# Seven products of quarters instead of eight in the second FFN's up projection

## The chip, the cores and the metric

The kernel runs on one core of one Trainium2 chip. Its metric is the device time of one execution in microseconds; the number that counts is the median of several runs. The core has a matrix engine (TensorE, PE in the rows, with its weight loads as PEld), three engines for element-wise work (VectorE, DVE; ScalarE, ACT; GpSimd, POOL), and an engine that issues the DMAs (SyncE, SP).

## The reference

The kernel computes a two-layer block over 512 latent tokens and 256 context tokens of 1024 channels, in float32. Layer 0 mixes by two convolutions, layer 1 by windowed attention; each is followed by a feed-forward network (FFN). The change is in the FFN of layer 1, which runs on the 512 latent tokens alone:

```
def conv_ffn(h, w_up, conv, w_down):
    u = dwconv(h @ w_up, conv)          # h: 512 x 1024, w_up: 1024 x 5632, three taps along the tokens
    a, g = jnp.split(u, 2, axis=-1)     # 2816 features each
    return (jax.nn.silu(g) * a) @ w_down
```

## The kernel before

Channels or features lie on the 128 partitions, tokens along the free dimension. `h` is 8 channel tiles of 512 tokens. The 5632 features of the up projection are 44 tiles of 128: pair f (0 to 21) is feature tile f of the half a and of the half g.

Every product in float32 is made of three: each operand is split into a high and a low part of at most twelve bits (`split`, lines 156 to 159: a cast on ScalarE, line 158, and a subtraction on VectorE, line 159), and `mm3` (lines 173 to 178) adds low x high, high x low and high x high into one accumulator in PSUM. So a feature tile of the up projection takes 8 channel tiles x 3 matmuls of 512 columns. Weights come by `weights` (line 161): a DMA of 128 x 1024 into one of three `wraw` buffers, then the split.

The second FFN is `ffn(1, ...)` from line 652, in the order of the program:

- The tokens come in two halves of 256. `output` and `tokens_in_turn` make `h` of the first half, then of the second (`mod_in`, line 330, with its VectorE and ScalarE steps), and prepare the weights of the first six feature tiles (pairs 0 to 2). `side_by_side` (line 200) makes these six for the first half of the tokens and then for the second, while `h` of the second half is still being made.
- `self.todo` holds the rest of the modulation: eight rows, each a DMA of 512 KB and a reduction on VectorE (line 253), which the gate of the down projection needs.
- `up(f)` (line 685) makes the two tiles of a pair, the weights one tile ahead; then three taps of the convolution for each tile (`conv3`: the middle tap out of PSUM by ScalarE, line 367, the two others by VectorE, line 369, their input in PSUM too), SiLU on ScalarE, the product on VectorE (line 704), and the split of the result g.
- `down(grp)` (line 707) projects a group of g back: groups are pairs 0–3, 4–7, 8–11, 12–16, 17–21. The projection of a group is written after the first pair of the next group. It has 8 output tiles of 4 or 5 x 3 matmuls of 512 columns, each with its own weights, and adds the gated result to x on VectorE (line 359). The last group's projection goes in two halves of tokens with the final norm.

Accumulators are eight PSUM slots of 512 columns, taken in turn. The order on each engine is not only that of the program: a planner goes through the instructions by its own estimates of their times, and gives an engine the first one in program order that it holds to be ready. `issue_after` ties an instruction behind another on its engine. Semaphores are then set for that order, and each engine's queue runs strictly in it.

## Time and profile before

| | us |
|---|---|
| median of 3 runs | 1493.58 |
| all runs | 1493.09, 1493.58, 1495.0 |
| span of the profiled execution | 1491.3 |
| TensorE busy | 1456.9 |
| VectorE busy | 1023.7 |
| ScalarE busy | 594.9 |
| GpSimd busy | 47.1 |

The profile is of one execution. Its span goes from the first to the last instruction; the page has no other time for that execution, and the median of the runs is 2.3 us above the span. A row of a timeline has the start and the duration of an instruction; of instructions that follow each other without a gap the next one starts some 0.07 us before the duration of the last one is over, so the time that an instruction takes up on its engine is read from start to start. The second FFN lies between 1109 us and the end.

### The profile page before, as it was taken

How to read it: one execution, taken by the hardware profiler on the slowest of the kernel's cores; microseconds unless marked ns; L12 is line 12 of the kernel's file. 1: busy time of each engine (PE TensorE's matmuls, PEld its weight loads, DVE VectorE, ACT ScalarE, POOL GpSimd, SP SyncE). 2: the span in 40 equal slices, each digit the busy share in tenths (PEclk: the TensorE clock that was granted, in tenths of full speed). 3: DMA queues.
4: the chain of work that ended last, by engine and by line, in shares of the span. 5: the costliest groups of instructions: out<-in, count | busy, mean ns of one | idle time of the engine just before them, and what ended most of it. 6: DMA issues, size and time to landing. Idle time of an engine off the chain costs nothing.

```text
span 1491.3 us, 21938 instructions
## 1 busy us (share of the span) xinstructions
PE 1456.9 (98%) x8786; PEld 1236.1 (83%) x8786; DVE 1023.7 (69%) x1635; ACT 594.9 (40%) x983; POOL 47.1 (3%) x186
## 2 busy tenths in 40 slices
PE   5999999999999999999999999999999999999998
PEld 4888888888888888888888878868799888888887
DVE  6699998679877756456434679786676854655455
ACT  5421224463213223123122376686664442424235
POOL 0000001110000000000000010110000000000000
PEclk9999999999999999999999999999999999999999
DMA  9314434034543532342211324011154333233222
GB/s 374 113 61 170 156 114 136 30 105 148 163 131 124 184 99 85 108 133 82 88 44 44 98 79 141 10 43 51 45 176 162 94 105 104 79 108 95 93 77 75
DMA packets 52709, 161.23 MB, mean 108 GB/s; under 512 B 6400, under 2 KB 6528, under 8 KB 52480
## 3 DMA queue, kind: packets, MB, share of 16 engines
q1 hardware_dynamic: 52608, 159.84, 32.6%
q8 instruction: 68, 1.11, 0.3%
q14 instruction: 33, 0.27, 0.1%
HBM read 155.10 MB, written 2.10 MB: 105 GB/s over the span
## 4 chain that ended last, share of the span: by engine, by line
PE 91%; DVE 3%; DMA 2%; ACT 2%; issue 1%; POOL 0%; DVEq 0%; ACTq 0%
PE slot L176 22%; PE slot L177 21%; PE slot L178 21%; PE av L177 3%; PE av L176 3%; PE av L178 3%; PE av L928 2%; PE pt L918 2%; PE s L899 2%; PE pt L176 2%; PE pt L177 2%; PE pt L178 2%; PE slot L225 1%; PE slot L211 1%; PE slot L207 1%; PE slot L208 1%
## 5 line engine op out<-in xcount | busy, mean ns | idle before, releaser
L176 PE MATMUL slot<-h,wlo 128*128 128x512 f32 (+1 forms) x1192 | 414.9, 350 | 2.2 <-DVE ub L569 1.1
L178 PE MATMUL slot<-h,whi 128*128 128x512 f32 (+1 forms) x1192 | 415.5, 349 | 0.0
L177 PE MATMUL slot<-h,whi 128*128 128x512 f32 (+1 forms) x1192 | 415.1, 349 | 0.2 <-DVE h L349 0.2
L158 ACT CAST whi<-wraw 128x1024 fp32r<-128x1024 f32 (+2 forms) x215 | 191.8, 900 | 210.6 <-PE slot L178 110.4
L176 PEld LDWEIGHTS slot<-h,wlo 128*128 128x128 f32 x1192 | 224.1, 188 | 37.3 <-issue 1.8
L177 PEld LDWEIGHTS slot<-h,whi 128*128 128x128 f32 x1192 | 225.1, 189 | 31.7 <-DVE h L349 0.5
L178 PEld LDWEIGHTS slot<-h,whi 128*128 128x128 f32 x1192 | 225.1, 189 | 30.5
L159 DVE TENSOR_TENSOR wlo<-wraw,whi 128x1024 fp32r<-128x1024 f32 (+2 forms) x215 | 222.0, 1038 | 23.8 <-ACT whi L158 23.3
L369 DVE SCALAR_TENSOR_TENSOR cf<-slot,par,cf 128x769 f32<-128x769 f32 (+1 forms) x132 | 122.0, 927 | 146.6 <-ACT cf L367 146.1
L176 PE MATMUL slot<-gh,wlo 128*128 128x512 f32 (+1 forms) x459 | 157.5, 344 | 0.4 <-DVE x L359 0.4
L367 ACT ACTIVATE cf<-slot,par 128x770 f32<-128x770 f32 (+1 forms) x66 | 55.0, 834 | 256.7 <-PE slot L178 244.1
L177 PE MATMUL slot<-gl,whi 128*128 128x512 f32 (+1 forms) x459 | 156.7, 342 | 0.0
L178 PE MATMUL slot<-gh,whi 128*128 128x512 f32 (+1 forms) x459 | 156.2, 341 | 0.0
L359 DVE SCALAR_TENSOR_TENSOR x<-slot,mod,x 128x256 f32<-128x256 f32 (+1 forms) x139 | 81.8, 617 | 81.0 <-PE slot L178 80.8
L577 DVE SCALAR_TENSOR_TENSOR cacc<-ub,par,cacc 128x783 f32<-128x783 f32 x120 | 118.3, 1035 | 0.2
L253 DVE CUSTOM_DVE_ANT_0 junk<-wmod,cb 128x1024 bf16<-128x1024 f32 x80 | 97.5, 1219 | 9.4 <-DMA wmod<-in_wmt 5.8
L176 PEld LDWEIGHTS slot<-gh,wlo 128*128 128x128 f32 x459 | 86.4, 189 | 12.3 <-issue 0.7
L177 PEld LDWEIGHTS slot<-gl,whi 128*128 128x128 f32 x459 | 86.6, 189 | 10.9 <-issue 0.2
L178 PEld LDWEIGHTS slot<-gh,whi 128*128 128x128 f32 x459 | 86.7, 189 | 10.5
L906 DVE CUSTOM_DVE_ANT_0 sm<-s,mask,nsink 128x640 f32<-128x640 f32 (+1 forms) x58 | 46.8, 819 | 16.0 <-PE pt L918 12.4
L703 ACT ACTIVATE sgf<-cf 128x770 f32<-128x770 f32 (+1 forms) x44 | 32.6, 741 | 61.3 <-DVE cf L369 61.1
L909 ACT ACTIVATE sm<-sm,nm 128x513 f32<-128x513 f32 (+1 forms) x64 | 50.0, 785 | 10.3 <-DVE nm L906 5.4
(244 smaller groups left out, 2247.0 us busy)
## 6 DMA issues: line engine op xcount, KB each, us to landing
wraw<-in_w_up SPq DMA_DIRECT2D x88, 512.0 KB, 3.4
wmod<-in_wmt SPq DMA_DIRECT2D x56, 512.0 KB, 3.9
wmod<-in_wm SPq DMA_DIRECT2D x40, 512.0 KB, 4.9
wraw<-in_w_down SPq DMA_DIRECT2D x48, 256.0 KB, 2.7
wraw<-in_w_in SPq DMA_DIRECT2D x20, 512.0 KB, 4.1
wraw<-in_w_down SPq DMA_DIRECT2D x32, 320.0 KB, 3.0
wraw<-in_w_o SPq DMA_DIRECT2D x16, 512.0 KB, 3.3
wraw<-in_w_out SPq DMA_DIRECT2D x16, 256.0 KB, 3.5
```

Of the source, the lines that this page charges most:

```text
L158: self.act_mark = self.nc.scalar.copy(hi, src)
L159: self.mark = self.nc.vector.tensor_tensor(lo, src, hi.bitcast(F32), op=ALU.subtract)
L176: mm(out, lo, xh, start=first, stop=False)
L177: mm(out, hi, xl, start=False, stop=False)
L178: self.product = mm(out, hi, xh, start=False, stop=last)
L253: nc.vector.tensor_tensor_reduce(junk, w, self.cb[:, c, :], 1.0, 0.0, ALU.mult, ALU.add, col)
L359: self.nc.vector.scalar_tensor_tensor(self.x[k][:, lo:hi], acc, self.mod[:, l, chunk * 8 + k, c:c + 1], self.x[k][:, lo:hi], op0=ALU.mult, ...
L367: nc.scalar.activation(acc[:, :n], u[:, :n], AF.Copy, scale=w[:, 1:2])
L369: nc.vector.scalar_tensor_tensor(acc[:, o], u[:, i], w[:, j:j + 1], acc[:, o], op0=ALU.mult, op1=ALU.add)
L577: self.tapped = nc.vector.scalar_tensor_tensor(acc, ub[:, t:t + CB_N], w[:, t:t + 1], acc, op0=ALU.mult, op1=ALU.add)
L906: scored = nc.vector.tensor_tensor_reduce(sm[:, :n], s[:, SEQ - nl:SEQ + CTX], mk, -SCALE, nsink[:, hd:hd + 1], ALU.add, ALU.min, nm)
L909: self.scored = scored, nc.scalar.activation(sm[:, :n + 1], sm[:, :n + 1], AF.Exp, scale=-1.0, bias=nm, accum_out=z)
```

## The change

For pairs 3 to 21 the up projection is written as a product of a 2 x 2 matrix of weight quarters and a 2 x 2 matrix of quarters of `h`: features of a or of g, by even or odd channel tiles, by the first or the second 256 tokens. The eight products of quarters (each 4 channel tiles x 3 matmuls of 256 columns) become Strassen's seven (in Winograd's form), of sums of quarters.

- `quarters` makes the sums of quarters of `h` once, from the unsplit `h`, which `mod_in` now writes into tiles that are kept (`raw`): for each of four pairs of channel tiles one subtraction of 512 elements, two of 256, and two splits of 512. It stands in the program before the rows of the modulation and before `side_by_side`.
- `load_seven` loads a pair's weights (one DMA of 512 KB and two of 256 KB) and makes four sums of weight quarters of 512 elements, two on VectorE and two on GpSimd.
- `split_seven` splits the seven weight quarters: three times 128 x 1024, once 128 x 512. The splits for the next pair are written between the products of the current one (`then`).
- `seven` makes the seven products in three PSUM slots of 256 columns, and combines them into two tiles in SBUF (`ua`, `ug`): four copies out of PSUM by ScalarE, three additions or subtractions with one operand in PSUM by VectorE. One accumulator takes up four of the products, and is read by ScalarE or VectorE between one and the next; another takes two. The three taps then read these tiles.
- The down projection's weights use two pairs of buffers in turn instead of up to five, and other buffers in the last projection. The loaded weights of these pairs are laid out with even channel tiles before odd ones. The scratch for dynamic DMAs is set to 1024 bytes.

Pairs 0 to 2 and all of layer 0 keep their operations. The diff also takes comments out, which is left out here:

```diff
...
-    def mm3(self, out, w, k, xh, xl, first, last):
+    def mm3(self, out, w, k, xh, xl, first, last, more=False):
         hi, lo = (t[:, k * P:(k + 1) * P] for t in w)
-        mm = self.nc.tensor.matmul
+        mm = partial(self.nc.tensor.matmul, skip_group_check=more)
...
-    def mod_in(self, h, k, r, n, l, shift, segs):
+    def mod_in(self, h, k, r, n, l, shift, segs, raw=None):
...
-        t = self.tmp.tile([P, T], F32, name="ht", tag="tC")
+        t = self.tmp.tile([P, T], F32, name="ht", tag="tC") if raw is None else raw(k, lo)
...
+    def load_seven(self, f):
+        nc = self.nc
+        w = self.a["w_up"][1][f]
+        ra, rb, rc = (self.wts.tile([P, 1024], F32, name="wraw", tag="wraw", bufs=3) for _ in range(3))
+        rd = self.ph.tile([P, 512], F32, name="wrd", tag="wrd")
+        nc.sync.dma_start(ra, w[0])
+        nc.sync.dma_start(rd, w[1][:, 512:])
+        nc.sync.dma_start(rc[:, 512:], w[1][:, :512])
+        nc.vector.tensor_tensor(rc[:, :512], ra[:, :512], ra[:, 512:], op=ALU.add)
+        nc.vector.tensor_tensor(ra[:, 512:], ra[:, 512:], rd, op=ALU.add)
+        nc.gpsimd.tensor_tensor(rb[:, :512], ra[:, 512:], ra[:, :512], op=ALU.add)
+        nc.gpsimd.tensor_tensor(rb[:, 512:], rb[:, :512], rc[:, 512:], op=ALU.add)
+        return ra, rb, rc, rd
+    def seven(self, f, parts, h, then):
+        nc = self.nc
+        xa, va, ya = (self.slot()[:, :256] for _ in range(3))
+        ua, ug = (self.ph.tile([P, SEQ], F32, name=n, tag=f"{n}{f % 2}") for n in ("ua", "ug"))
+        q = lambda t, i: t[:, 256 * i:256 * i + 256]
+        b = {n: [(q(x[0], i), q(x[1], i)) for x in src] for n, src, i in (
+            ("11", h[0::2], 0), ("21", h[1::2], 0), ("22", h[1::2], 1),
+            *((n, list(zip(self.th, self.tl)), i) for i, n in enumerate(("n1", "t3", "n2", "t4"))))}
+        lo, hi = slice(0, 256), slice(256, 512)
+        def product(acc, w, n, start=False):
+            for k in range(4):
+                self.mm3(acc, w, k, *b[n][k], start and k == 0, k == 3, not start)
+        (a11, s1), (s2, s4), (s3, a12), (a22,) = parts
+        product(xa, a11, "11", True)
+        nc.scalar.copy(ua[:, lo], xa)
+        product(va, s1, "n1", True)
+        nc.scalar.activation(ug[:, hi], va, AF.Copy, scale=-1.0)
+        then(0)
+        product(xa, s2, "n2")
+        nc.scalar.copy(ua[:, hi], xa)
+        product(va, s4, "22")
+        then(1)
+        product(xa, s3, "t3")
+        nc.vector.tensor_tensor(ug[:, hi], ug[:, hi], xa, op=ALU.subtract)
+        product(ya, a12, "21", True)
+        then(2)
+        product(xa, a22, "t4")
+        then(3)
+        nc.vector.tensor_tensor(ua[:, hi], ua[:, hi], va, op=ALU.add)
+        nc.vector.tensor_tensor(ua[:, lo], ua[:, lo], ya, op=ALU.add)
+        nc.scalar.activation(ug[:, lo], xa, AF.Copy, scale=-1.0)
+        return ua, ug
+    def late(self, i):
+        return [self.act.tile([P, DM], F32R, name=f"{t}{i}") for t in ("whi", "wlo")]
+    def quarter_room(self, p):
+        return [pool.tile([P, 1024], F32R, name=t, tag=f"{t}{p}") for t, pool in (("th", self.act), ("tl", self.ph))]
+    def halves(self, hi, lo):
+        return (hi[:, :512], lo[:, :512]), (hi[:, 512:], lo[:, 512:])
+    def split_seven(self, raws, i, first=False):
+        raw = raws[i]
+        if first:
+            out = []
+            for j in range(2):
+                hi, lo = (self.ph.tile([P, SEQ], F32R, name=t, tag=f"{t}{4 + j}") for t in ("gh", "gl"))
+                self.split(raw[:, 512 * j:512 * j + 512], hi, lo)
+                out.append((hi, lo))
+            return out
+        if i == 3:
+            hi, lo = (self.act.tile([P, DM], F32R, name=f"{t}2")[:, :512] for t in ("whi", "wlo"))
+            self.split(raw, hi, lo)
+            return [(hi, lo)]
+        hi, lo = (self.wts.tile([P, 1024], F32R, name=t, tag=t, bufs=3) for t in ("whi", "wlo"))
+        self.split(raw, hi, lo)
+        return self.halves(hi, lo)
...
-        # the first tiles take the first tokens while the others are not there yet
+        if l:
+            self.quarters()
         self.do(11 if l else 3)
         done = [self.slot() for _ in self.pre]
         self.side_by_side(done, h, segs)
         nf = len(done)
-        with self.tc.issue_after(self.marks[0].ins), self.tc.issue_after(self.marks[1].ins):
-            ahead = self.weights(a["w_up"][l, ups[nf][0], ups[nf][1]], into=self.spare(0))
+        if l == 0:
+            with self.tc.issue_after(self.marks[0].ins), self.tc.issue_after(self.marks[1].ins):
+                ahead = self.weights(a["w_up"][l, ups[nf][0], ups[nf][1]], into=self.spare(0))
+        else:
+            raws = self.load_seven(nf // 2)
+            self.parts = [self.split_seven(raws, i, i == 0) for i in range(4)]
         g = []
 
         def up(f):
-            nonlocal ahead
+            nonlocal ahead, raws
             acc = []
+            if l and 2 * f >= nf:
+                now = self.parts
+                if f + 1 < NF:
+                    raws = self.load_seven(f + 1)
+                    self.parts = []
+                def then(i):
+                    if f + 1 < NF:
+                        self.parts.append(self.split_seven(raws, i))
+                u = self.seven(f, now, h, then)
             for part in range(2):
                 i = 2 * f + part
                 if i < nf:
                     s = done[i]
+                elif l:
+                    s = u[part]
                 else:
                     w = ahead
                     if i + 1 < len(ups):
...
 
         def down(grp):
             for m in range(KT):
-                w = self.weights(a["w_down"][l][grp][m], len(GROUPS[grp]) * P, self.spare(m % 3) if m % 3 < 2 else None)
+                room = (self.spare(m % 3) if m % 3 < 2 else None) if l == 0 else self.late(m % 2)
+                w = self.weights(a["w_down"][l][grp][m], len(GROUPS[grp]) * P, room)
                 s = self.slot()
                 self.wide_gemm(s, w, g[GROUPS[grp][0]:GROUPS[grp][-1] + 1], whole)
                 for lo, hi in whole:
...
         for grp, fs in enumerate(GROUPS):
             for f in fs:
                 up(f)
-                # the last tile of a group is ready once the next group's first product is through
                 if grp and f == fs[0]:
                     down(grp - 1)
         self.do(len(self.todo))
...
             t = self.ph.tile([P, 2, DM], F32R, name="wcb", tag="cb")
             return t[:, 0, :], t[:, 1, :]
 
-        room = {4: partial(self.spare, 0), 5: partial(self.spare, 1), 7: cb}
-        room[6] = partial(self.spare, i, n, ("gh", "gl")) if l == 0 else partial(self.spare, 2)
+        if l == 0:
+            room = {4: partial(self.spare, 0), 5: partial(self.spare, 1), 7: cb}
+            room[6] = partial(self.spare, i, n, ("gh", "gl"))
+        else:
+            room = {4 + p: partial(self.quarter_room, p) for p in range(4)}
         project = self.project(wd, len(last) * P, last, segs, l, 5, lead=2, late=6, few=(2, 4), room=room)
         if l == 0:
             self.tokens_in_turn(segs, project, (2, 1, 0), [a["w_k"][0], a["w_k"][1], a["w_q"][0]])
...
                 slots = self.turned(segs[1])
             self.final(segs[1], slots, y1)
 
...
+        self.raw = [self.act.tile([P, 1024], F32, name="raw", tag=f"th{p}") for p in range(KT // 2)]
+        def raw(k, lo):
+            t = self.raw[k // 2]
+            if k % 2 == 0:
+                return t[:, 0:512]
+            return t[:, 768:1024] if lo == 0 else t[:, 256:768]
         half = self.project(a["w_o"], DM, o, HALVES[1:], 1, 2, few=(1, 3))
-        self.tokens_in_turn(HALVES, half, (3, 1, 3), [w[f, part] for f in range(3) for part in range(2)], 0, room)
+        self.tokens_in_turn(
+            HALVES, half, (3, 1, 3), [w[f, part] for f in range(3) for part in range(2)], 0, room, raw)
+        self.room = room
+    def quarters(self):
+        nc = self.nc
+        self.th, self.tl = [], []
+        for p, raw in enumerate(self.raw):
+            b = raw.rearrange("p (q n) -> p q n", q=4)
+            t, u = (self.tmp.tile([P, T], F32, name="qs", tag=g)[:, :SEQ] for g in ("tA", "tB"))
+            nc.vector.tensor_tensor(
+                t.rearrange("p (q n) -> p q n", q=2), b[:, 0:3:2, :], b[:, 1:2, :].broadcast_to([P, 2, 256]), op=ALU.subtract)
+            nc.vector.scalar_tensor_tensor(u[:, :256], t[:, :256], -1.0, b[:, 2, :], op0=ALU.mult, op1=ALU.subtract)
+            nc.vector.scalar_tensor_tensor(u[:, 256:], u[:, :256], -1.0, b[:, 3, :], op0=ALU.mult, op1=ALU.subtract)
+            hi, lo = self.quarter_room(p)
+            for i, src in enumerate((t, u)):
+                self.split(src, hi[:, 512 * i:512 * i + 512], lo[:, 512 * i:512 * i + 512])
+            self.th.append(hi)
+            self.tl.append(lo)
 
...
+    even_odd = d["w_up"][1, 3:].reshape(NF - 3, 2, P, KT // 2, 2, P).transpose(0, 4, 2, 1, 3, 5)
+    d["w_up"][1, 3:] = even_odd.reshape(NF - 3, 2, P, DM)
...
+    nc = bacc.Bacc("TRN2", target_bir_lowering=False, num_devices=1, dynamic_dma_scratch_size=1024)
```

## Rows read from the trace of the kernel before

**Rows 1.** Page, part 1: busy us and share of each engine over the span.

```profile
PE 1456.9 (98%) x8786; PEld 1236.1 (83%) x8786; DVE 1023.7 (69%) x1635; ACT 594.9 (40%) x983; POOL 47.1 (3%) x186
```

**Rows 2.** Busy time by stretch of the second FFN: us, then each engine's busy time (instructions).

```profile
1144.30:1166.99 22.69, 22.37 (x97) 17.85 (x96) 21.23 (x33) 12.66 (x20) 0.00 (x0) 1.00 0.50 154
...
1166.99:1450.00 283.01, 283.00 (x1223) 229.23 (x1222) 160.20 (x209) 97.39 (x136) 0.00 (x0) 1.00 0.30 94
```

**Rows 3.** Chain of waits from 1118 us: start, us, what.

```profile
1148.97 1.15 DVE wlo L159
```

**Rows 4.** Timeline of TensorE, second FFN: start, us, line, operation, out<-in.

```profile
1106.14 0.28 PE L176 MATMUL slot<-oh,wlo 128*128 128x256 f32 x1
...
1108.99 0.28 PE L207 MATMUL slot<-h,wlo 128*128 128x256 f32 x1
...
1155.14 0.40 PE L176 MATMUL slot<-h,wlo 128*128 128x512 f32 x1
...
1166.29 0.40 PE L176 MATMUL slot<-h,wlo 128*128 128x512 f32 x1
...
1172.77 0.63 PE L176 MATMUL av<-gh,wlo 128*128 128x512 f32 x2
```

**Rows 5.** Timeline of VectorE, back-to-back instructions at two places.

```profile
190.08 2.92 DVE L577 SCALAR_TENSOR_TENSOR cacc<-ub,par,cacc 128x783 f32<-128x783 f32 x3
192.91 0.95 DVE L600 TENSOR_TENSOR ya<-slot,acca 128x770 f32<-128x770 f32 x1
...
1148.88 1.22 DVE L159 TENSOR_TENSOR wlo<-wraw,whi 128x1024 fp32r<-128x1024 f32 x1
1150.02 1.40 DVE L369 SCALAR_TENSOR_TENSOR cf<-slot,par,cf 128x511 f32<-128x511 f32 x2
1151.34 1.22 DVE L159 TENSOR_TENSOR wlo<-wraw,whi 128x1024 fp32r<-128x1024 f32 x1
```

**Rows 6.** Timelines of GpSimd and VectorE where both work: a sum, then small operations.

```profile
193.07 1.89 POOL L583 TENSOR_TENSOR cs<-cacc 128x783 f32<-128x783 f32 x1 [149.98 <-DVE cacc L577]
...
193.78 2.96 DVE L577 SCALAR_TENSOR_TENSOR cacc<-ub,par,cacc 128x783 f32<-128x783 f32 x2
...
197.53 1.97 DVE L577 SCALAR_TENSOR_TENSOR cacc<-ub,par,cacc 128x783 f32<-128x783 f32 x2
...
1118.97 1.23 DVE L159 TENSOR_TENSOR wlo<-wraw,whi 128x1024 fp32r<-128x1024 f32 x1 [0.34 <-ACT whi L158]
...
1119.04 1.21 POOL L298 TENSOR_TENSOR rt<-rt,rv 128x2 f32<-128x2 f32 x1
...
862.59 2.79 POOL L298 TENSOR_TENSOR rt<-rt,rv 128x2 f32<-128x2 f32 x1
...
866.29 0.20 POOL L298 TENSOR_TENSOR rt<-rt,rv 128x2 f32<-128x2 f32 x1
...
864.03 0.68 DVE L349 TENSOR_TENSOR h<-ht,h 128x512 fp32r<-128x512 f32 x1
864.64 0.68 DVE L335 TENSOR_TENSOR xr<-x,r 128x512 f32<-128x512 f32 x1
```

**Rows 7.** ScalarE's groups by form: busy us, mean ns of one, then idle before.

```profile
L158 ACT CAST whi<-wraw 128x1024 fp32r<-128x1024 f32 x135 | 140.7, 1045 | 123.2 <-PE slot L178 65.2 <-DMA wraw<-in_w_up 39.4 <-issue 7.9
...
L367 ACT ACTIVATE cf<-slot,par 128x512 f32<-128x512 f32 x22 | 15.2, 689 | 45.9 <-PE slot L178 37.8 <-PE slot L211 8.1
...
L826 ACT COPY v<-slot 128x256 f32<-128x256 f32 x6 | 2.2, 363 | 1.4 <-PE slot L824 1.4
```

**Rows 8.** Page, part 6: DMA issues, KB each, median us to landing.

```profile
wraw<-in_w_down SPq DMA_DIRECT2D x48, 256.0 KB, 2.7
```

**Rows 9.** Timeline of VectorE, head of the second FFN.

```profile
1133.53 0.43 DVE L159 TENSOR_TENSOR h<-ht,h 128x256 fp32r<-128x256 f32 x1 [0.77 <-ACT h L158]
1135.90 1.22 DVE L253 CUSTOM_DVE_ANT_0 junk<-wmod,cb 128x1024 bf16<-128x1024 f32 x1 [1.95 <-ACT cb L665]
...
1177.89 0.68 DVE L159 TENSOR_TENSOR gl<-sgf,gh 128x512 fp32r<-128x512 f32 x1
```

More of the change, by code (lines that the diff above doesn't have):

```diff
@@ L351, in mod_in, with modulated @@
             self.split(t[:, lo:hi], h[k][0][:, lo:hi], h[k][1][:, lo:hi])
[L353 removed]
+    def modulated(self, h, r, n, l, shift, seg, raw=None):
         for k in range(KT):
[L355 removed]
+            self.mod_in(h, k, r, n, l, shift, [seg], raw)
     def gate_in(self, k, acc, l, chunk, lo, hi):
@@ L506, in layer0_output, with tokens_in_turn @@
         self.tokens_in_turn(segs, project, (1, 0, 3), [up[0, 0], up[0, 1], up[1, 0]], 3)
-    def tokens_in_turn(self, segs, project, norm, first, early=1, room=()):
+    def tokens_in_turn(self, segs, project, norm, first, early=1, room=(), raw=None):
         self.pre = [self.weights(w) for w in first[:early]]
```

7 lines of the change are left out of this document (2 added, 5 removed).

## Prediction

> **What bounds the kernel now.** I read the page's busy shares first, then the stretches of the second FFN, then the chain of waits, then the engines' timelines there. The page [rows 1] shows TensorE busy 98% of the span of 1491.3 us; the reader should see that VectorE is not idle beside it: 69% over all. By stretch [rows 2], between 1144.3 and 1167.0 us, where the second FFN has its six first tiles done and makes pairs 3 and 4, VectorE is busy 21.2 of 22.7 us, and over the rest, to 1450.0, 160.2 of 283.0. TensorE is busy throughout, at a granted clock of 1.00. So the stage is bound by the number of columns that TensorE streams, with VectorE close behind at its head. The chain of waits [rows 3] says the same: its last link outside TensorE before the tail is a split of weights on VectorE, from 1148.97 us; behind it stand matmuls alone.
>
> **What is removed: TensorE time.** A pair of tiles takes 48 matmuls of 512 columns; from 1155.14 to 1166.29 us [rows 4] that is 11.15 us, 0.232 each. After: 7 products x 4 tiles x 3 parts = 84 matmuls of 256 columns. Twenty-four of these, each with a weight load of its own as here, took 2.85 us from 1106.14 to 1108.99 [rows 4], 0.119 each: 10.0 us a pair. The shorter matmul already includes whatever its weight load costs, so the loads (84 for 48) are no further term. Saved: 1.15 us x 19 pairs (3 to 21) = 21.9 us, if TensorE never waits.
>
> **What is added on VectorE.** I take start-to-start times of back-to-back instructions, since a row's duration overlaps the next one's [rows 5]: 0.61 us for 512 elements of two SBUF tensors (864.03 to 864.64, rows 6), 1.14 for 1024 (1148.88 to 1150.02), so 0.34 for 256 by the slope; 0.66 for a tap of the FFN's convolution (two from 1150.02 to 1151.34). Taps now read SBUF instead of PSUM; three such of 783 elements took 2.83 us (190.08 to 192.91), 0.943 each, by the same slope 0.66 at 511, so no change. A pair then has two weight sums 1.22, three splits of 1024 and one of 512 4.03, three accumulations out of PSUM 1.02, four taps 2.64, product and split of g 1.22: 10.1 us. Before it was 2.28 + 2.64 + 1.22 = 6.1 of 11.15. So VectorE alone now needs as long as TensorE (10.0).
>
> **What is added on GpSimd, and its price on VectorE.** Two sums of 512 elements a pair. The one large GpSimd sum in the trace, 783 elements, took 1.89 us [rows 6], so 512 take about 1.24. That row also shows the price: it began at 193.07; the two taps that VectorE began at 193.78 took 2.96 us, where the two at 197.53 took 1.97. VectorE lost 0.99 of the 1.18 us that the sum still had. The other way round [rows 6], a product of two elements on GpSimd, 0.20 us alone (866.29), took 1.21 beside one split of 1024 (1118.97) and 2.79 beside VectorE's unbroken work, until 865.3. The two engines exclude each other on two-SBUF-tensor work. 1.12 us (1.24 x 1.70/1.89) is what a sum would cost VectorE from its first moment; where it starts beside an accumulation out of PSUM (one SBUF operand; the product at 192.91 [rows 5], one operand in PSUM, kept its 0.87 us to the next start) less. I take 0.95 a sum. Bounds: 0, if the sums find VectorE idle, and 3.7 us a pair, rival 2. A pair in steady state: 10.1 + 1.9 = 12.0 us, longer than the 11.15 of before.
>
> The Trainium skill ("SBUF — State Buffer", section "Who interferes with whom") speaks against the change in the same way: a VectorE instruction with two SBUF inputs and a GpSimd instruction that reads SBUF share a port, and whichever starts first blocks the other for its whole length. The trace agrees in kind (0.99 us lost, 2.79 for 0.20). By the rule in full, 1.24 a sum, a pair would take 12.6, twelve pairs of the runs below 0.6 us more each, and the time would be near 1512.
>
> **ScalarE and DMA.** ScalarE gets four casts of at most 1.05, four copies of 256 columns at 0.36, and keeps the pair's first taps, SiLU and g, four of about 0.69 [rows 7]: 8.4 us of 10, hidden. Each copy must end before its accumulator is used again one product (1.43 us) later; alone it does, queued behind a cast of 1.05 just about. Bytes are the same, 1 MB a pair. Queue: in SP's order the pair's DMAs (first rows whole, second in two halves) stand behind the release of raw buffers. The quarter d is released by its split at the start of a pair; cast and split at most 1.05 + 0.68, landing 2.7 for 256 KB, sum 0.68, cast 1.05, split 1.22 make 7.4 us [rows 5 to 8] before the next pair can start. Of the 2.6 us left I give 1.1 to hand-overs and queues: VectorE may lag 1.5 us in a run of pairs before TensorE stops.
>
> **The sum by stretch.** The projections down stand after pairs 4, 8, 12, 17, and VectorE has slack there; the last pair's convolution (3.84) and its sums fall into it. So pairs come in runs. The first of a run needs 6.24 + 1.90 on VectorE, less than TensorE's 10.0; the others 12.0.
> - Pairs 5–8 and 9–12: 10.0 + 3 x 12.0 - 1.5 = 44.5 each; 13–17: 56.5; 18–21, where nothing is loaded for a pair after the last: 10.0 + 24.0 + 10.0 - 1.5 = 42.5. Together 188.0 against 17 x 11.15 = 189.6: -1.6 us. Bounds: -19.6 at TensorE's pace, +18.8 at 13.7 us a pair.
> - Head. VectorE ends the last tile of h at 1133.9 [rows 9], TensorE the side-by-side tiles at 1144.3. What VectorE then has until g of pair 3 is ready: quarter sums of h, per pair of channel tiles 0.61 + 2 x 0.39 + 2 x 0.61 = 2.6, four of them 10.4; eight modulation rows at 1.22 [rows 9] 9.8; three splits of pair 3 2.9; sums and splits of pair 4 with GpSimd's share 7.1; four convolutions 15.4; three accumulations 1.0. Together 46.6: 1180.5 us. TensorE has pairs 3 and 4 until 1164.3 and, with weights for two tiles (the change leaves two buffers), 18 matmuls of the projection down, 4.2 us. The full start of that projection moves from 1167.0 [rows 2] to 1180.5 - 4.2 = 1176.3: +9.3. Before, this queue was full too (a split of g still starts at 1177.89 [rows 9]), but with enough other products ready to fill TensorE. Bounds: +2 (some quarter sums before 1133.9, GpSimd free) to +16 (VectorE stops for its operands, as for 1.95 us ahead of 1135.90 [rows 9]).
> - Three later projections down: the first weights' raw buffer is freed only by the next pair's first split; TensorE can fill with the next pair, but in VectorE's order. I take 1 us each, +3; bounds 0 to 8.
> - Tail after 1450 us and all that lies ahead of 1109: nothing; the freed DMA scratch and the other rooms change no operation. Bounds 0 to 3.
>
> Sum: -1.6 + 9.3 + 3 = +10.7 us. The profiled execution's span is 1491.3 [rows 1]: 1502.0. The median of the three runs, 1493.6, lies 2.3 above that span, which I add as what lies around it: **1504 us**.
>
> **Rivals.**
> 1. TensorE's pace holds: GpSimd's sums fall into gaps and beside PSUM reads, VectorE's 10.1 fit. Runs -19.6, head +4, projections +1: 1479 us. For it: 10.1 to 10.0 is nearly even, and the planner fills gaps, as in before at 1172.77, where it takes up a third accumulator of the projection down before the last parts of the others [rows 4]. Against: the loss in rows 6, and that a balanced loop leaves VectorE no gaps. It decides from the steady pair's time: twelve pairs of the runs carry it, so the whole comes out even at 12.0 - 10.7/12 = 11.1 us with the forecast's head, and at 11.7 with this rival's.
> 2. Starved sums: GpSimd gets in only when VectorE's queue is stopped by the very split that waits for the sums (as the 2.79 us row). Then two sums (2.48), a cast (1.05) and a hand-over (some 0.1) stand in line with VectorE: 10.1 + 3.6 = 13.7 a pair. Runs +18.8, head +14, projections +6: 1532 us. Against: three PSUM accumulations a pair let GpSimd in.
> 3. It does not do what it says in the plan: the planner mixes pairs and projections so well that VectorE's slack there is used up too (96 matmuls at 0.23 are 22 us, against 8 x 1.27 of splits and gates and 5 left over: 7 us each). Then it ends midway between the forecast and rival 1: 1492, no change.
>
> Chances: forecast 0.45 (own range 1492 to 1518), rival 1 0.25, rival 2 0.22, rival 3 0.08. The change is slower in most of the forecast's cases and all of rival 2's. What a measurement of this kernel can tell from no change is 0.2%, 3 us. Faster: 0.24 of rival 1, 0.04 of the forecast, 0.02 of rival 3: 0.30. Same: 0.10. Slower: 0.60. Leaving out a tenth at each side: 1477 to 1535.
>
> **What would show it.** Right: in the runs of pairs VectorE busy without a gap, TensorE with waits on the split wlo and on g after 1144 us; GpSimd's sums longer than 1.24 us where VectorE has two-tensor work; the first projection down some 10 us late. Rival 1: TensorE busy throughout, pairs 10.0 us apart. Rival 2: VectorE waiting for ScalarE's cast behind GpSimd in each pair. Wrong altogether if a 256-column matmul with these weights does not run at 0.119 us, or if TensorE waits somewhere outside the second FFN.

## The result and the profile after

The changed kernel takes 1552.61 us (median of 4 runs, 1551.78 to 1553.57) against 1493.34 of the kernel before beside it: a ratio of 1.0394 [1.0379, 1.0409]. The forecast was 1504 with a range of 1477 to 1535; the sign was right, the time lies 48.6 us above it. The profiled execution took 1551.78 us, its span is 1550.0 (before 1491.3 [rows 1]).

The page's busy times (share of the span, instructions):

```profile
PE 1453.4 (94%) x9470; PEld 1264.5 (82%) x9470; DVE 1132.5 (73%) x1789; ACT 653.8 (42%) x1106; POOL 111.1 (7%) x224
```

TensorE is busy 94% instead of 98, and VectorE, with 108.8 us more work, 73%: neither is full. By stretch (window; length, busy time and count of PE, PEld, DVE, ACT, POOL; granted clock; DMA share; GB/s), first the two stretches that answer to [rows 2], then the way from one projection down to past the next, and last the whole:

```profile
1144.00:1170.00 26.00, 12.02 (x93) 10.99 (x91) 24.54 (x38) 16.23 (x25) 3.46 (x2) 0.91 0.38 126
1170.00:1190.00 20.00, 12.63 (x84) 12.22 (x84) 19.96 (x28) 8.29 (x14) 2.79 (x2) 0.84 0.27 86
1190.00:1215.00 25.00, 23.55 (x112) 19.88 (x113) 12.88 (x20) 7.24 (x13) 0.00 (x0) 0.88 0.38 116
1215.00:1260.00 45.00, 40.77 (x312) 38.69 (x311) 37.89 (x52) 22.84 (x39) 10.79 (x7) 1.00 0.23 71
1260.00:1305.00 45.00, 38.38 (x220) 33.61 (x219) 29.93 (x40) 16.83 (x29) 5.16 (x4) 0.92 0.28 88
1144.00:1505.00 361.00, 300.61 (x1988) 274.13 (x1987) 279.36 (x375) 164.52 (x268) 60.67 (x36) 0.94 0.28 88
```

To 1190 us VectorE is full (44.5 of 46) and TensorE busy half the time. Behind it VectorE has room (12.9 of 25, 37.9 of 45), and TensorE still stands; and its granted clock, 1.00 throughout before, lies below that in all of these stretches but one. What TensorE waited for (line, tile; in all, times, longest):

```profile
PE slot L177 <- DVE wlo L159: 21.1, 6, 10.3
PE pt L177 <- DVE wlo L159: 12.9, 4, 6.6
PE av L177 <- DVE wlo L159: 9.3, 3, 6.6
PE slot L177 <- DVE ug L695: 8.1, 6, 2.3
PE pt L177 <- ACT ua L686: 3.3, 3, 1.1
PE slot L177 <- ACT ua L686: 2.2, 2, 1.1
PE pt L177 <- DVE ug L695: 1.6, 2, 1.1
PE av L177 <- DVE ug L695: 1.0, 2, 0.5
```

Two kinds: split weights (wlo, 43.3 us) and the reuse of an accumulator that has not been read yet (ug by VectorE 10.7, ua by ScalarE 5.5, together 16.2). TensorE's timeline says where the large ones stand (start, duration, ..., wait ahead of it):

```profile
1170.53 0.58 PE L177 MATMUL slot<-h,wlo 128*128 128x256 f32 x1 [10.28 <-DVE wlo L159]
1191.45 0.79 PE L177 MATMUL pt<-gh,wlo 128*128 128x512 f32 x1 [5.95 <-DVE wlo L159]
1268.00 0.79 PE L177 MATMUL slot<-gh,wlo 128*128 128x512 f32 x1 [6.62 <-DVE wlo L159]
1344.01 0.79 PE L177 MATMUL pt<-gh,wlo 128*128 128x512 f32 x1 [6.60 <-DVE wlo L159]
1432.54 0.80 PE L177 MATMUL av<-gh,wlo 128*128 128x512 f32 x1 [6.56 <-DVE wlo L159]
```

One is the start of pair 4; the other four are the first matmul (input gh) of each of the four projections down ahead of the last. The chain that ends at the second of them, in order of time (start, duration, what):

```profile
1254.17 3.50 DMA wrd<-in_w_up
...
1257.69 0.70 DVE wraw L664
...
1258.62 1.85 POOL wraw L665
...
1260.54 2.14 POOL wraw L666
...
1264.59 0.61 ACT whi L158
...
1265.53 2.43 DVE wlo L159 x3
...
1268.00 0.79 PE slot L177
1268.79 0.43 PE slot L178
1269.22 0.43 PE slot L179
...
1271.23 0.23 PE slot L178
```

This is the next pair's preparation: its quarter d lands, VectorE's sum, GpSimd's two, cast, splits; only then, in VectorE's order, the split for the projection. And that projection's weights came late anyway, for their raw buffer was one of the three that the next pair held (SyncE's queue: three issues spread over 5.49 us, as buffers come free):

```profile
1261.60 5.49 SPq L164 DMA_DIRECT2D wraw<-in_w_down  x3
```

Pair 8 had ended on TensorE at 1261.4, and the split of the next pair's first weights (1259.56, 1.98 us) was over at 1261.5: TensorE could have begun pair 9 (24 matmuls, 2.9 us; the weights behind these were split near 1265.6), but the projection stands first in its order. Behind the wait the matmuls of 512 columns come 0.43 us apart instead of 0.23, the lower of the clock's two levels (1.2 GHz), until 1271.2; ahead of it those of 256 columns came 0.12 us apart, the upper level (granted clock 1.00 from 1215 to 1260).

So the account has three terms. The columns go by count, 1.15 us for each pair made by seven products. For the rest I sum TensorE's rows from 1146 us to 31 us ahead of the last sum of squares: start to start, less the wait in the row, less 0.119 us for 256 columns and 0.232 for 512. After: **21.9 us fewer columns, 60.3 us of waits, 17.8 us of matmuls slower than at the full clock**, together +56.2 of the span's +58.7. By place:

| | before | after | shift | forecast shift |
|---|---|---|---|---|
| first projection down starts | 1166.99 | 1191.45 | +24.5 | +9.3 |
| second | 1234.09 | 1268.00 | +33.9 | +10.2 |
| third | 1300.69 | 1344.01 | +43.3 | +11.1 |
| fourth | 1378.49 | 1432.54 | +54.1 | +12.8 |
| last sum of squares | 1482.07 | 1540.57 | +58.5 | +10.7 |

### The profile page after: what moved, and what is told of

The parts are those of the page before. It is cut to its first block, busy times and chain, and to the rows that moved or that the text cites. A ratio compares the mean times of both kernels' runs of the same rounds, so it can differ in the third digit from the quotient of the medians.

```text
span 1550.0 us, 23843 instructions
## 1 busy us (share of the span) xinstructions
PE 1453.4 (94%) x9470; PEld 1264.5 (82%) x9470; DVE 1132.5 (73%) x1789; ACT 653.8 (42%) x1106; POOL 111.1 (7%) x224
## 4 chain that ended last, share of the span: by engine, by line
PE 78%; DVE 10%; DMA 4%; ACT 3%; POOL 3%; issue 2%; SPq 0%; POOLq 0%; DVEq 0%; ACTq 0%
PE slot L177 19%; PE slot L178 19%; PE slot L179 19%; DVE wlo L159 3%; PE av L1034 2%; PE pt L1024 2%; PE s L1005 2%; DMA wrd<-in_w_up 2%; PE av L177 2%; PE av L178 2%; PE pt L177 2%; PE av L179 2%; PE pt L178 1%; PE pt L179 1%; ACT whi L158 1%
## 5 line engine op out<-in xcount | busy, mean ns | idle before, releaser
L177 PE MATMUL slot<-h,wlo 128*128 128x256 f32 (+1 forms) x1144 | 384.4, 338 | 15.7 <-DVE wlo L159 13.0
L179 PE MATMUL slot<-h,whi 128*128 128x256 f32 (+1 forms) x1144 | 384.3, 336 | 0.0
L178 PE MATMUL slot<-h,whi 128*128 128x256 f32 (+1 forms) x1144 | 384.0, 336 | 0.2 <-DVE h L350 0.2
L158 ACT CAST whi<-wraw 128x1024 fp32r<-128x1024 f32 (+2 forms) x230 | 208.2, 915 | 289.0 <-PE slot L179 126.0
L159 DVE TENSOR_TENSOR wlo<-wraw,whi 128x1024 fp32r<-128x1024 f32 (+2 forms) x230 | 249.4, 1092 | 22.3 <-ACT whi L158 22.0
L177 PEld LDWEIGHTS slot<-h,wlo 128*128 128x128 f32 x1144 | 215.6, 189 | 44.6 <-DVE wlo L159 13.8
L178 PEld LDWEIGHTS slot<-h,whi 128*128 128x128 f32 x1144 | 216.7, 189 | 24.8 <-DVE h L350 0.5
L179 PEld LDWEIGHTS slot<-h,whi 128*128 128x128 f32 x1144 | 216.7, 189 | 23.4
L370 DVE SCALAR_TENSOR_TENSOR cf<-slot,par,cf 128x769 f32<-128x769 f32 (+1 forms) x92 | 92.3, 1005 | 116.7 <-ACT cf L368 116.6
L177 PE MATMUL slot<-gh,wlo 128*128 128x512 f32 (+1 forms) x444 | 153.8, 348 | 7.0 <-DVE wlo L159 6.6
L368 ACT ACTIVATE cf<-slot,par 128x770 f32<-128x770 f32 (+1 forms) x46 | 41.2, 895 | 210.9 <-PE slot L179 206.4
L177 PE MATMUL slot<-th,wlo 128*128 128x256 f32 x152 | 43.7, 287 | 11.9 <-DVE ug L695 8.1
```

The lines of the kernel that those rows point to most:

```text
L158: self.act_mark = self.nc.scalar.copy(hi, src)
L159: self.mark = self.nc.vector.tensor_tensor(lo, src, hi.bitcast(F32), op=ALU.subtract)
L177: mm(out, lo, xh, start=first, stop=False)
L178: mm(out, hi, xl, start=False, stop=False)
L179: self.product = mm(out, hi, xh, start=False, stop=last)
L368: nc.scalar.activation(acc[:, :n], u[:, :n], AF.Copy, scale=w[:, 1:2])
```

## The experiments

Each was run beside the kernel before on the same chip. Theories A and B are those of the recorded expectation of each run. The last three columns are the same account for each, from its own trace (a few us of each span lie outside that stretch). "DVE" in a name: GpSimd's sums made by VectorE.

| run | pairs by seven | median us | ratio to before | columns | waits | slow matmuls |
|---|---|---|---|---|---|---|
| after | 3–21 | 1552.6 | 1.0394 [1.0379, 1.0409] | -21.9 | 60.3 | 17.8 |
| e_rd | 3–21 | 1536.4 | 1.0286 [1.0271, 1.0302] | -21.9 | 46.0 | 16.6 |
| e_draw | 3–21 | 1521.0 | 1.0185 [1.0170, 1.0200] | -21.9 | 32.5 | 15.5 |
| e_both | 3–21 | 1519.4 | 1.0169 [1.0152, 1.0186] | -21.9 | 32.7 | 13.9 |
| e_dvesums | 3–21 | 1541.0 | 1.0318 [1.0303, 1.0334] | -21.9 | 47.7 | 21.2 |
| f_both_dve | 3–21 | 1512.9 | 1.0128 [1.0113, 1.0143] | -21.9 | 26.0 | 13.4 |
| f_nopool | 3–21 | 1508.9 | 1.0100 [1.0086, 1.0113] | -21.9 | 25.8 | 10.7 |
| f_nosums | 3–21 | 1495.9 | 1.0016 [1.0007, 1.0026] | -21.9 | 18.6 | 4.7 |
| f_n5 | 5–21 | 1516.9 | 1.0152 [1.0135, 1.0169] | -19.6 | 27.7 | 13.9 |
| f_n5_dve | 5–21 | 1511.2 | 1.0115 [1.0100, 1.0130] | -19.6 | 18.8 | 13.7 |
| h_both_room | 3–21 | 1513.7 | 1.0136 [1.0121, 1.0152] | -21.9 | 26.7 | 13.5 |
| g_alt | 7 of them | 1502.4 | 1.0058 [1.0046, 1.0071] | -8.1 | 9.9 | 4.7 |
| g_alt_pool | 7 of them | 1502.1 | 1.0056 [1.0042, 1.0070] | -8.1 | 9.6 | 7.2 |
| g_two3 | 10 of them | 1508.3 | 1.0096 [1.0082, 1.0110] | -11.5 | 14.7 | 6.6 |
| h_alt9 | 6 of them | 1495.1 | 1.0007 [0.9998, 1.0016] | -6.9 | 4.6 | 2.0 |
| h_full9 | 9–21 | 1506.2 | 1.0083 [1.0069, 1.0097] | -15.0 | 13.6 | 8.8 |
| i_three | 3 of them | 1494.3 | 1.0006 [0.9997, 1.0015] | -3.5 | 1.9 | 0.9 |
| i_late | 6 of them | 1487.9 | 0.9963 [0.9950, 0.9977] | -6.9 | 1.4 | -0.2 |
| j_full_late | 3–21 | 1498.0 | 1.0028 [1.0019, 1.0038] | -21.9 | 17.0 | 6.3 |

**Buffers: e_rd, e_draw, e_both.**

```diff
-        rd = self.ph.tile([P, 512], F32, name="wrd", tag="wrd")
+        rd = (self.tmp.tile([P, 512], F32, name="wrd", tag="rd", bufs=1) if f % 2 and f > 4
+              else self.ph.tile([P, 512], F32, name="wrd", tag="wrd"))      # e_rd, e_both
...
+                raw = self.ph.tile([P, DM], F32, name="wraw", tag=("cb", "wmod")[m % 2]) if l else None
-                w = self.weights(a["w_down"][l][grp][m], len(GROUPS[grp]) * P, room)
+                w = self.weights(a["w_down"][l][grp][m], len(GROUPS[grp]) * P, room, raw)   # e_draw, e_both
```

> A second buffer for the quarter d from pair 5 on (every other pair's, in room that the modulation rows have left). Theory A (a circle through buffers): a steady pair takes 12.6 us because the DMA of the next d waits for the split of this one, which VectorE does only after both GpSimd sums, so that sum, GpSimd's two sums, cast, splits and DMA stand in one circle. With two buffers the stops of VectorE on that DMA (0.6 and 1.2 us in two pairs looked at) go, about 1 us in each of some 12 pairs: 1540 us, pairs near 11.5. Theory B (VectorE's load): VectorE with GpSimd beside it needs the 12 us itself and the stops on the DMA only show that it is ahead for a moment: at most 3 us, 1550.

> The down projection's weights get two raw buffers of their own (in the room of the modulation rows), so that their DMA no longer waits for the buffers of the next pair. Theory A: the four waits of 6.0 to 6.6 us ahead of the projections fall below 1 us, and the stretches at half clock behind them (24 matmuls in 7.2 to 7.8 us where 5.6 would do) go with them: 4 x 7 = 28 us, 1525. Theory B: the split of these weights still stands in VectorE's queue behind the splits of the next pair; only the DMA's 3 us go: 12 us, 1541, and about 3 us are left at each projection's start.

> Both at once: second buffer for the quarter d, own raw buffers for the down projection's weights. Theory A: 12 + 28 = 40 us, 1512. Theory B: 15 us, 1537. Neither gives back the 18 us between the end of the first six tiles and the first down projection that are not the wait for its weights.

e_draw gives 31.6 us back by itself, near theory A's 28: the largest single gain of one edit. It need not all be the earlier DMA: the planner orders TensorE anew for these buffers. In after the second projection begins behind pair 8; in e_draw its first 24 matmuls lie in pieces among the products of the pairs from 6 on, and the first of them waits for nothing. The first projection still waits for its weights, for less:

```profile
1182.47 0.51 PE L177 MATMUL pt<-gh,wlo 128*128 128x512 f32 x1 [1.63 <-DVE wlo L159]
...
1227.40 0.39 PE L177 MATMUL slot<-gh,wlo 128*128 128x512 f32 x1
```

How much is the DMA and how much the new order was not separated. e_rd gives 16.2, more than A's 12.6, and not as it said: the run of pairs that precedes the second projection takes as long as in after (273 matmuls in 38.4 us, in after 38.1), and what went are the waits ahead of three projections (6.6 to 1.2 and twice 2.0; ahead of the first it grew to 8.9), probably since the next pair's splits are over sooner. The two cure the same waits, so together they give 33.2 and not 40, and both theories' sums for e_both miss.

**The sums: e_dvesums, f_both_dve, f_nopool, f_nosums.**

```diff
-        nc.gpsimd.tensor_tensor(rb[:, :512], ra[:, 512:], ra[:, :512], op=ALU.add)
-        nc.gpsimd.tensor_tensor(rb[:, 512:], rb[:, :512], rc[:, 512:], op=ALU.add)
+        nc.vector.tensor_tensor(rb[:, :512], ra[:, 512:], ra[:, :512], op=ALU.add)      # e_dvesums, f_both_dve
+        nc.vector.tensor_tensor(rb[:, 512:], rb[:, :512], rc[:, 512:], op=ALU.add)
...
+        nc.sync.dma_start(rb, w[0])             # f_nopool, f_nosums: instead of GpSimd's sums
+        nc.sync.dma_start(rc, w[1])             # f_nosums: instead of VectorE's sums
```

> GpSimd's two sums made by VectorE instead. VectorE gets 1.2 us a pair more of its own and loses what GpSimd's sums lengthened its work by (a split 1.98 where it takes 1.21 elsewhere, two taps 1.76 where they take 1.46). Theory A: the circle is shorter by 1.84 + 2.13 - 1.3 = 2.7 us, the pair falls by 1 us to VectorE's own 11.6: some 12 us, 1540. Theory B with the lock as price: VectorE's sum is about even (+1.2 - 1.1): 1550 to 1554. If GpSimd took real load off VectorE: 1565, 1.2 us in each of 12 pairs more.

> Both buffers (as e_both), and GpSimd's two sums made by VectorE. With the buffers free, what is left between 1170 and 1510 us should be VectorE's load. Theory A (the lock is the price): VectorE does two sums of 0.61 us a pair itself and is rid of some 1.8 us of lengthened instructions: 0.6 us x 18 pairs = 11 us, 1508. Theory B (what is left are waits by the order, not load): within 3 us of e_both's 1519. If GpSimd does relieve VectorE: 1.2 us x 18 = 22 us more, 1541.

> Both buffers as in e_both, and GpSimd's two sums left out (the buffer is loaded with the unsummed first row of weights instead, so two of the seven products take wrong weights; VectorE keeps its two sums). Measures the price of the two sums by itself: by the prediction's step GpSimd costs VectorE 0.95 us a sum, 1.9 a pair, as much as or more than making them there (1.22). So theory A (the lock is the price, where VectorE sets the time): as far below e_both's 1519 as VectorE's lost time, some 15 us, 1504, and 9 below f_both_dve's 1513. Theory B (the sums matter by the line sum, cast, split in which they stand): they cost the same on either engine up to their length, so 1509 to 1513.

> Both buffers, and no sums of weight quarters at all (the three buffers are loaded as they are, so the products are of other weights than they should be; everything else stays). Theory A (VectorE's load): VectorE is rid of 3.0 us a pair, 54 us in all, and TensorE's idle time between 1170 and 1510 us, 22 us in e_both, goes, and the clock's losses with it (some 5): 1492. What is then left against 1471 (1493 less 22 for the columns) is the head. Theory B (order): 1512 or more.

f_nopool and f_nosums multiply weights that were not summed, and load 512 and 768 KB more a pair. From 1519.4 (e_both, whose own runs lie some 6 us apart), with both buffers: GpSimd's two sums left out 10.5 us less, the same two on VectorE 6.5 less, all four left out 23.5 less. So on GpSimd these sums cost some 10.5 us, on VectorE 4.0, and VectorE's own two 13.0, the added DMA included. e_dvesums and f_nosums come out near theory A (1540, 1492); f_both_dve lies between the two theories, f_nopool at the lower end of B (1509 to 1513): VectorE's load is part of what is left, not all. The rows of VectorE from 1215 to 1500 us and of GpSimd from 1130 to 1510 (shape; busy, mean ns | idle before), first of after, then VectorE's of f_both_dve:

```profile
L159 DVE TENSOR_TENSOR wlo<-wraw,whi 128x1024 fp32r<-128x1024 f32 x47 | 64.8, 1390 | 5.5 <-ACT whi L158 5.5
L370 DVE SCALAR_TENSOR_TENSOR cf<-ua,par,cf 128x511 f32<-128x511 f32 x32 | 31.9, 996 | 0.0
...
L806 DVE TENSOR_TENSOR sgf<-sgf,cf 128x512 f32<-128x512 f32 x15 | 11.4, 762 | 2.3 <-ACT sgf L805 2.3
L159 DVE TENSOR_TENSOR gl<-sgf,gh 128x512 fp32r<-128x512 f32 x15 | 11.3, 754 | 2.1 <-ACT gh L158 2.1
...
L666 POOL TENSOR_TENSOR wraw<-wraw 128x512 f32<-128x512 f32 x18 | 32.1, 1782 | 1.4
L665 POOL TENSOR_TENSOR wraw<-wraw 128x512 f32<-128x512 f32 x18 | 28.6, 1588 | 309.1 <-DVE wlo L159 132.3 <-DVE wraw L664 129.9 <-ACT gh L158 35.1
```

```profile
L159 DVE TENSOR_TENSOR wlo<-wraw,whi 128x1024 fp32r<-128x1024 f32 x45 | 54.8, 1223 | 8.2 <-ACT whi L158 7.9
...
L370 DVE SCALAR_TENSOR_TENSOR cf<-ua,par,cf 128x511 f32<-128x511 f32 x32 | 23.9, 747 | 0.0
L159 DVE TENSOR_TENSOR gl<-sgf,gh 128x512 fp32r<-128x512 f32 x17 | 11.7, 688 | 1.5 <-ACT gh L158 1.4
L807 DVE TENSOR_TENSOR sgf<-sgf,cf 128x512 f32<-128x512 f32 x17 | 11.7, 687 | 0.0
```

Beside GpSimd the same VectorE instructions are longer: 47 x 0.17 + 32 x 0.25 + 15 x 0.075 + 15 x 0.066 = 18 us in that stretch, 0.6 us for each of GpSimd's 32 sums there. A sum that takes 0.69 on VectorE takes 1.6 to 1.8 on GpSimd. On VectorE it is the better in every pair of runs but one, g_alt and g_alt_pool, which are even; in g_alt VectorE is busy two thirds to three quarters of the time from 1200 us on.

**The head: f_n5, f_n5_dve, h_both_room.** In f_n5 pairs 3 and 4 are made as before the change, and the sums of quarters of h are written ahead of pair 4 instead of ahead of the first six tiles (in its trace they run from 1178.0 us, behind the start of the first projection).

```diff
-        if l:
-            self.quarters()
...
+            if l and f == 4:
+                self.quarters()
-            if l and 2 * f >= nf:
+            if l and f in range(5, NF):        # pairs 3 and 4: wide_gemm, weights one tile ahead
...
-                room = ... else self.late(m % 2)
+                room = ... else self.late(m % 3) if m % 3 < 2 else None      # h_both_room alone
```

> Both buffers, and the seven products only from pair 5 on: pairs 3 and 4 as before the change, the sums of quarters of h written ahead of pair 4 instead of ahead of the first six tiles. Theory A (the head is a queue on VectorE of quarter sums, modulation rows and the first two sets of splits, ahead of which TensorE stands 14 us and more): the head comes back to that of before but for the 10 us of quarter sums, which find room in the 45 us to the second projection; 18 to 20 us less, and 2.3 lost with the two pairs' columns: 1502. Theory B: VectorE is as full behind the head, and the quarter sums stop TensorE there instead: 1512 to 1518.

> The same with GpSimd's sums on VectorE. If the lock is the price there as well, the difference to f_n5 is that of f_both_dve to e_both (A: 10 us less, 1492, so even with the kernel before; B: no difference).

> f_both_dve (own raw buffers, second buffer for d, sums on VectorE), and the down projection's weights in three places in turn instead of two, as the kernel before had them. Theory A (the head's stop at the first projection down and the clock behind it come from having weights for two tiles only while g is late): the first projection fills more of the time in which VectorE is behind: 5 to 8 us less, 1506. Theory B (VectorE's queue at the head is the whole of it): within 2 us of 1513.

Against e_both and f_both_dve, f_n5 gives 2.5 us, f_n5_dve 1.7, h_both_room nothing: theory B for f_n5 and h_both_room. f_n5_dve is 5.7 us below f_n5, nearer to what the sums on VectorE gave without f_n5's edit (6.5) than to B's nothing, and far above A's 1492. f_n5 by stretch:

```profile
1144.00:1170.00 26.00, 23.75 (x104) 19.16 (x103) 22.97 (x35) 13.36 (x21) 3.85 (x2) 0.93 0.48 161
1170.00:1200.00 30.00, 23.36 (x105) 18.84 (x104) 28.77 (x45) 12.16 (x21) 4.47 (x2) 0.83 0.20 62
```

TensorE's 12.0 busy us of 1144 to 1170 have become 23.8, but now it stands 6.6 us of the next 30, at a clock of 0.83, beside a VectorE that is busy 28.8. By the same account, TensorE's waits from 1146 to 1200 us are 8.9 us where e_both has 15.1, but the slow matmuls 6.6 for 4.7, and two pairs' columns (2.3) are given up: the stop became shorter and later, and little was won. VectorE is busy 51.7 of these 56 us, in e_both 54.5.

**Fewer pairs: g_alt, g_alt_pool, g_two3, h_alt9, h_full9.** All with own raw buffers; the sums on VectorE but for g_alt_pool; g_two3 and h_full9 with the second buffer for d as well; h_alt9 and h_full9 with three places for the down projection's weights, as in h_both_room.

```diff
+SEVEN = (7, 9, 11, 13, 15, 18, 20)      # g_alt; g_two3: 7, 8, 10, 11, 13, 14, 16, 18, 19, 21
+                                        # h_alt9: without 7; h_full9: range(9, NF)
+            if l and f == 5:             # h_alt9, h_full9: 7
+                self.quarters()
+            if l and f in SEVEN:
```

> Seven products for every other pair only (7, 9, 11, 13, 15, 18, 20), the others as before the change; sums on VectorE, own raw buffers for the down projection, sums of quarters of h ahead of pair 5. Theory A (VectorE's load per pair is what eats the gain): two pairs need 10.1 + 1.2 + 6.1 = 17.4 us of VectorE for 21.2 of TensorE, so the saving of 1.15 x 7 = 8 us is kept but for some of the 10 us of quarter sums: 1485 to 1490, faster than before. Theory B (each of these pairs brings its own waits by its order: copies, accumulators, splits): 1496 to 1503.

> The same with the two sums on GpSimd. Theory A: where VectorE has 4 us to spare in two pairs, the lock costs little and the line through GpSimd (some 2.5 us longer) is hidden by the pair before: within 2 us of g_alt. Theory B: as g_alt or up to 7 us above it.

> Seven products for two of three pairs (7, 8, 10, 11, 13, 14, 16, 18, 19, 21), sums on VectorE, both buffers. Theory A: three pairs need 11.3 x 2 + 6.1 = 28.7 us of VectorE for 31.1 of TensorE, which still fits beside the projections' slack: 11.5 us saved, some stops: 1484 to 1490. Theory B: 1500 to 1507.

> g_alt with the seven products for pairs 9, 11, 13, 15, 18, 20 only, the sums of quarters of h ahead of pair 7, and three places for the down projection's weights. The whole head is then as before the change. Theory A (g_alt lost its 7 to 8 us of columns and 9 more in the head, where waits of 8.7 us and a clock of 0.89 stand between 1144 and 1200, and little behind it): 6 x 1.15 = 6.9 us saved, 2 to 4 lost to waits: 1489 to 1491, faster than before. Theory B (each pair by seven products brings its own waits of about what it saves): 1493 to 1497.

> As h_alt9, but the seven products for all pairs from 9 on (13 pairs), with both buffers. Theory A of VectorE's load: the runs of pairs at 11.3 us of VectorE to 10.0 of TensorE lose more than the columns save, so it is slower than h_alt9: 1494 to 1500, although it saves 15 us of columns.

All lie above what theory A gave them, except that g_alt_pool is within 2 us of g_alt, as A had it. g_two3 is above B too (1500 to 1507). In g_alt most of the loss stands in the head, where VectorE is full, with the sums of quarters of h among its work:

```profile
1170.00:1200.00 30.00, 25.07 (x97) 18.92 (x96) 29.97 (x51) 13.71 (x23) 0.00 (x0) 0.89 0.22 64
```

From 1146 to 1200 us it has 6.1 us of waits and 3.3 of slow matmuls, of 9.9 and 4.7 in all. Behind 1200, with VectorE busy 32.8, 35.2 and 36.5 of 50 us, it loses 5.2 of the 8.1 saved. h_alt9, whose head has 1.4 us of waits to 1200, is 7.3 us faster; but its account too is only even (-6.9, +4.6, +2.0), though VectorE is busy 71% from 1200 to 1450 us. The largest of its waits:

```profile
PE av L181 <- DVE gl L162: 1.8, 3, 0.9
PE pt L180 <- ACT gh L161: 0.8, 1, 0.8
PE pt L181 <- DVE gl L162: 0.7, 1, 0.7
```

They are for gh and gl: at a projection TensorE has done all parts but those of the group's last pair, whose g is not there yet. The pair in between, which covered that on the kernel before, is shorter on TensorE and has more VectorE work ahead of the g. The next experiment takes this up.

**The order: i_late, i_three, j_full_late.**

```diff
-                if grp and f == fs[0]:
+                if grp and f == fs[l and grp < 4]:      # i_late, j_full_late
```

i_late is h_alt9 with this line, j_full_late is f_both_dve with it: the first three projections stand one pair later. i_three is h_alt9 without it, with three pairs by seven (10, 14, 19).

> h_alt9 with each of the first three projections down written after the second pair of the next group instead of after the first, so that the g of the group's last pair has a pair's time more to be ready. Theory A (what is left of the price of these pairs are TensorE's waits for the last g, 3 us at three projections, and the half clock behind them, 2 us, because the pair by seven products is shorter on TensorE and longer on VectorE): waits fall to 1 us, 1489 to 1491. Theory B: TensorE runs out of other work somewhere else, 1493 to 1497.

> As h_alt9, with the seven products for three pairs only (10, 14, 19), one in each of the last three groups, away from the projections. Theory A: 3 x 1.15 = 3.5 us saved and next to nothing lost, since VectorE has slack all round: 1490 to 1491. Theory B (each brings its own price): 1493 to 1495.

> The change in full (pairs 3 to 21 by seven products) with all that helped: own raw buffers for the down projection's weights, second buffer for d, sums on VectorE, and the first three projections written one pair later. Against f_both_dve (1512.9). Theory A (order: the waits for the last g and the accumulators behind it are some 12 us in f_both_dve, and the half clock behind them some 5 more): 1497 to 1501. Theory B (VectorE's load: what does not wait for g waits for the next split): 1506 to 1513. Both leave it slower than the kernel before and than i_late, which uses a third as many of these pairs.

i_late is theory A, 1.1 us below its range, and the one version that beats both kernels: 1487.9 us, 0.37% below before. From 1144 to 1450 us TensorE is busy 304.6 of 306 us at a clock of 1.00 (before 305.7). All that it still waits for from 1140 us on:

```profile
PE slot L180 <- DVE wlo L162: 1.4, 1, 1.4
PE slot L294 <- DVE ss L287: 0.4, 1, 0.4
```

VectorE has no less to do than in h_alt9 (180.0 of 250 us from 1200 on, there 176.5), so it was the order, not VectorE's load, that cost h_alt9 its gain. The same line gives the full form 14.9 us: 1498.0, theory A again. j_full_late by stretch, and the largest group of its waits:

```profile
1144.00:1170.00 26.00, 13.48 (x92) 12.37 (x92) 25.22 (x41) 13.35 (x22) 0.00 (x0) 0.77 0.45 139
1170.00:1200.00 30.00, 29.27 (x193) 27.33 (x192) 29.02 (x47) 16.63 (x27) 0.00 (x0) 0.92 0.45 143
1200.00:1450.00 250.00, 246.17 (x1704) 228.34 (x1703) 218.63 (x322) 133.07 (x217) 0.00 (x0) 0.99 0.31 95
```

```profile
PE slot L177 <- DVE wlo L159: 10.5, 3, 8.6
```

Behind 1200 us TensorE is busy 98% with VectorE at 87%; what is lost is the head, 12.5 us of idle before 1170. i_three, which keeps the early projections, is even with before (3.5 us saved, 2.8 lost in the account): theory B.

## Why the prediction was wrong

- **The step that failed: "Three later projections down: the first weights' raw buffer is freed only by the next pair's first split; TensorE can fill with the next pair, but in VectorE's order. I take 1 us each, +3; bounds 0 to 8".** The cause was seen and mis-sized. TensorE could not fill: in its fixed order the projection's first matmul stood ahead of the next pair's, so DMA (2.7 us), cast and a place behind three splits in VectorE's queue stood open: 6.6 us three times, 5.95 at the first projection, with 24 matmuls behind each in 7.0 to 8.2 us instead of 5.6 (30 in 9.6 instead of 7.0). Where the sum had 3 us for the three later projections, they measured 19.8 of waits and 6.7 of slower matmuls. In the table of places, the shift grew by 9.4, 9.4 and 10.8 us from one projection to the next, where the forecast had 0.9, 0.9 and 1.7. e_draw's edit, which takes away just that sharing (the planner's new order comes with it), gave 31.6 us.
- **"at a granted clock of 1.00"** was used for the time after the change too. Stops bring the lower level, and the matmuls behind them cost 17.8 us more; the sum had no such term.
- **"Each copy must end before its accumulator is used again ... just about"** was priced at nothing: 5.5 us of waits on ScalarE's copy to ua. The larger part is VectorE's reading of an accumulator (ug, 10.7 us), which stood in no such line at all; the 1.5 us of lag that a run of pairs allowed VectorE did not cover it.
- **Head, +9.3, bounds to +16:** +24.5. The sum of VectorE's work, 46.6 us to g of pair 3 at 1180.5, was short by 4.8 (the last part of that split ended near 1185.3; 1.4 us ahead of 1145.65 were idle), and the projection's weights (5.95 us) came on top; I had counted 4.2 us of that projection as done ahead. That VectorE's queue is the head's cause fits its busy time (44.5 of 46 us), and that more places for weights give nothing (h_both_room); f_n5 shortened the stop and won little.
- **Steady pair 12.0 us:** 12.6 and 13.0 in the two looked at (1235.76 to 1248.37, then to 1261.4), near enough. GpSimd's price was in kind right, in size 0.6 instead of 0.95 us a sum, its sums 1.6 to 1.8 instead of 1.24. The line of 7.4 us before the next pair can start was wrong: it left out GpSimd's two sums and set d's split at the start of a pair. In the trace that split is the last of the four, at 1253.46 and again at 1266.67, 13.2 us apart. That this line sets the pair's time is not shown: with a second buffer for d (e_rd) the pairs took as long.
- **Right:** 84 matmuls at 0.119 us are 10.0 us a pair (with them i_late's account, which has hardly a stop, is left with -0.2 us); taps from SBUF cost what they cost from PSUM where GpSimd does not work beside them (0.75 us, 0.66 start to start); DMA bytes; ScalarE's busy time (42%) fits beside TensorE's, though its order cost the 5.5 us above.
- **Rivals.** Rival 2's 1532 was the nearest time, but VectorE was not starved as it had it: from 1215 to 1500 us it idled 6.5 us on ScalarE's casts and 7.0 on d's DMA. Its line through GpSimd was real; it was TensorE that stood behind it. Rival 3's "so well that no change" is what the better order (j_full_late) comes near, at +0.28%.

The Trainium skill ("Perfetto Trace Analysis", section "Optimization Strategy") says that the same gap repeating on an engine that should be saturated can mean that there is no room for the next tile. The trace agrees: four waits of 6 to 6.6 us stood at the same instruction, and with own buffers (e_draw) the longest wait for a projection's weights was 1.63 us. The Trainium skill ("SBUF — State Buffer", section "Who interferes with whom") says that a VectorE instruction with two SBUF inputs contends with a GpSimd instruction that reads SBUF, for a port that one of them holds alone. The longer rows on both sides (VectorE's splits 1390 ns for 1223; GpSimd's sums 1588 and 1782 ns on average, 1.26 us at best) agree in kind, at 0.6 us of VectorE a sum, half of what a full block would have been by the prediction's 1.24.

What stays open: in j_full_late the head's 12.5 us. That the modulation rows or a smaller first set of splits could give it back was not tried. Of e_draw's 31.6 us the part of the buffers and that of TensorE's new order were not separated. The parts of GpSimd's 10.5 us that are lock and that are length of line were not separated.

## What to carry to other kernels

Fewer matmul columns are worth only what the engines that feed them can follow: ask of each new buffer use who else holds that buffer, and at which instruction of TensorE's fixed order a late tile will stand. Price a stop of TensorE with the matmuls behind it, which run at the lower clock: here 0.25 to 0.75 us for each us of wait, in the runs with more than 4 us of waits. Where a trick costs the side engine more than it saves the main one, try it for some of the units, and move what depends on the late result by one unit: of the versions here only the one that did both (i_late) beat the kernel before.

## What the runs showed that was not expected

- TensorE's clock also falls in short stops close together. f_both_dve's TensorE timeline:

```profile
1319.25 0.72 PE L177 MATMUL pt<-gh,wlo 128*128 128x512 f32 x2 [0.88 <-ACT gh L158]
1321.43 0.80 PE L178 MATMUL pt<-gl,whi 128*128 128x512 f32 x1 [1.46 <-DVE gl L159]
1322.03 0.63 PE L179 MATMUL pt<-gh,whi 128*128 128x512 f32 x1
1322.45 0.63 PE L178 MATMUL pt<-gl,whi 128*128 128x512 f32 x1
```

  Behind the stop of 0.88 us two matmuls of 512 columns still took 0.72 us together; behind that of 1.46 they came 0.42 us apart (granted clock 0.50 from 1322 to 1326 us).
- Two cures of one wait: 16.2 and 31.6 us alone, 33.2 together.
- A GpSimd sum of 512 elements took 1.26 us at best and up to 2.2 in after; the same sum on VectorE 0.69.
